# A decoder layer on one core: sums moved from GpSimd to VectorE, the norm's factor applied late, and two DeltaNet units beside the merge's loads

## The chip, the cores and the metric

One core of a Trainium2 chip runs the whole program. The time is that of one launch on the device, in microseconds (us). The engines are TensorE (PE, with PEld for its weight loads), VectorE (DVE), ScalarE (ACT), GpSimd (POOL) and SyncE (SP). In this kernel all transfers are issued by SP, in order.

## The reference

One layer of a decoder trunk with two mixers side by side, sequence 1024, width 1024, float32:

```
h   = RMSNorm(x);  p = h @ W_in
y_dn = GatedDeltaNet(p) @ W_dn      # 8 heads of 128, chunks of 64
y_ns = NSA(p) @ W_nsa               # 16 heads of 64; compressed, selected, window branches
x   = x + (sigmoid(g_dn) * y_dn + sigmoid(g_ns) * y_ns) @ W_out
x   = x + relu(RMSNorm(x) @ W_up)^2 @ W_down      # inner width 4096
```

RMSNorm(x) is x / sqrt(mean(x^2) + eps) * gain, over the width.

## The kernel before, in words

Activations lie transposed: the width on partitions, in 8 pieces c of 128, the sequence in two halves of 512. A matmul of two float32 operands is done as three: each operand is split into a high part (a copy by ScalarE, `wh`, `hh`, `ah`) and a low part (a subtraction on VectorE, `wl`, `hl`, `al`), and hi·hi, hi·lo and lo·hi go into the same PSUM bank. `split` (L184) and `parts` (L273) make the pair, `unit` (L280) loads two 128x512 tiles of weights and splits them. A scheduler puts the instructions of each engine in an order; priorities are the program's order and tables of steps (`at`, `at3`) where stages are mixed.

Start: x is loaded, made into hh and hl, and its squares are summed (`x_sums`, L334 and L335), partly on GpSimd. A root (`root_rows`, L244) takes eight one-column matmuls per row block, the mean on VectorE (L241), the power -1/2 on GpSimd (L242), a diagonal on VectorE (L252, `rd` or `tmp`) and a matmul that spreads it. Then come the DeltaNet heads, and the NSA attention with the DeltaNet output projection between its steps: `dn_part` multiplies, `dn_gate` (L1351 to L1353) loads a gate tile `th`, applies it and stores the result to `mxd`. The buffer `th` has one place, so the second gate is loaded after the first is stored.

Merge: `ns_rows` loads and splits the attention's rows `o`, `ns_merge` multiplies them with `w_pn`, gates the product and adds `mxd`'s tile (`md`). It can begin when the PSUM pools of the attention are shut and `pq` is opened. Output projection: `out_proj(half, c)`, 16 products, adds x, stores x1 (`x1d`), sums the squares. Norm: `norm_first` and `norm_second` multiply x1 by gain and root and form seven combinations of its four blocks, B11, B21, T2, T3, T4, T1, B22, each split in two.

MLP up and down use a Winograd scheme: a 2x2 block product in seven products p instead of eight. For the up product n = 0 to 15 and each product is 12 matmuls; `weights_of` makes the left side from the blocks a11, a12, a21, a22, two of its three sums on GpSimd (L1451 with no engine given, L1514); `up_out` applies relu and the square; `up_sums` forms the sums that the down product takes as its other side and stores them to `acd`. In the down product, 2 x 56 products are run in the order of `turns`, with sides prepared LEAD = 4 products ahead: w_d's blocks on the left, `acd`'s tiles (`bb`, split to `ah`, `al`) on the right, results added to x1 (L1664).

Of the kernel before, what the change touches and what calls it, by code (L numbers as in the profile page):

```python
# [146 lines left out]
def body(ctx: ExitStack, tc: tile.TileContext, A, out):  # L147
# [74 lines left out]
    for half in range(2):  # L222
        for k in range(8):
            xs.append(PL.pa.tile([128, 512], F32, name=f"x{half}{k}"))
            SY.dma_start(xs[-1], A["x"][k, :, half * 512:(half + 1) * 512])
        if half == 0:
            load_consts(cp, 0)
            cp_raw = [wp.tile([128, 4, 128], F32, name="wr", bufs=3) for _ in range(2)]
            for i in range(2):
                SY.dma_start(cp_raw[i], A["w_cp"][0][:, 4 * i:4 * i + 4])  # L230
# [49 lines left out]
    def unit(src):  # L280
        ks = []
        for i in range(2):
            wr = wp.tile([128, 4, 128], F32, name="wr", bufs=3)
# [42 lines left out]
    def x_sums(half):  # L326
        sa = [PL.pa.tile([128, 512], F32, name=f"sa{i}") for i in range(2)]
        for k in range(8):
# [5 lines left out]
            (GP if half or k >= 4 else V).tensor_tensor(sa[k // 4], sa[k // 4], sq, OP.add)  # L334
# [34 lines left out]
    for k in range(8):  # L369
        x_part(1, k)  # L370
    proj(p_cp, CX["w", 0], 0)
# [95 lines left out]
    def cmp_hidden(u, i):  # L467
# [3 lines left out]
        w1 = wp.tile([128, 4, 128], F32, name="wr", bufs=3)  # L471
# [72 lines left out]
    at(2, 2, cp_prep, 1)  # L544
# [371 lines left out]
    def fill_nb(u):  # L916
# [3 lines left out]
        def prep():  # L920
            for kp in range(4):
                wr = wp.tile([128, 2, 256], F32, name="wr", bufs=3)
# [415 lines left out]
    def dn_part(half, c, j):  # L1338
        oh, ol = D_["o", half]
        ks = D_["w", half, c]  # L1340
        if j == 0:
            D_["y"] = PL.ga.tile([128, 512], F32, name="g")
# [5 lines left out]
    def dn_gate(half, c):  # L1348
        sl = slice(half * 512, half * 512 + 512)
        th = PL.pr.tile([128, 512], F32, name="th", bufs=1)  # L1350
        SY.dma_start(th, gtd[c, :, sl])  # L1351
# [25 lines left out]
    shut("po", "pm", "pT", "pS", "ga", "pr")  # L1377
    pool("pf", 4, side="right")
    bank("pq", 4)
# [18 lines left out]
    def ns_merge(c, half):  # L1398
# [14 lines left out]
    ns_rows(0)  # L1413
    for c, half in [(0, 0), (1, 0), (0, 1), (1, 1)] + [(c, half) for c in range(2, 8) for half in range(2)]:
# [7 lines left out]
    x1, sums = [[], []], [None, None]  # L1422
# [3 lines left out]
    def out_proj(half, c):  # L1426
# [9 lines left out]
        SY.dma_start(x1d[c, :, HALF[half]], x)  # L1436
        if c == 0:
            sums[half] = t512(PL.p5, "u", 4)
            act(sums[half], x, AF.Square)
        else:  # L1440
            sq = t512(PL.pw, "tmp", 2)
            act(sq, x, AF.Square)
            (V if half else GP).tensor_tensor(sums[half], sums[half], sq, OP.add)
# [6 lines left out]
    def sub(o, a, b, eng=None):  # L1450
        (eng or GP).tensor_tensor(o, a, b, OP.subtract)  # L1451
# [3 lines left out]
    def parts_of(n, src, i, eng=V):  # L1455
        act(R[n][:, i], src)
        sub(R[n][:, 4 + i], src, f(R[n][:, i]), eng)

    def norm_first(r):
        R["raw"] = raw = f(big(False))  # L1460
        R["B11"], R["B21"] = big(True), big(True)
        for k in range(8):
            V.scalar_tensor_tensor(raw[:, k], x1[0][k], cols[:, 8 + k:9 + k], r, op0=OP.mult, op1=OP.mult)
            parts_of("B21" if k >= 4 else "B11", raw[:, k], k % 4)

    def norm_second(r):
        raw = R["raw"]
        R["T2"], R["T3"] = big(True), big(True)
        b12, b22, t = [], [], []

        def head(j):
            b12.append(t512(PL.p5, "b", 4))
            V.scalar_tensor_tensor(b12[j], x1[1][j], cols[:, 8 + j:9 + j], r, op0=OP.mult, op1=OP.mult)
            sub(raw[:, j], b12[j], raw[:, j], V)
            b22.append(t512(PL.p5, "c", 8))
            V.scalar_tensor_tensor(b22[j], x1[1][4 + j], cols[:, 12 + j:13 + j], r, op0=OP.mult, op1=OP.mult)

        def second(j):
            t.append(t512(PL.p5, "c", 8))
            sub(t[j], b22[j], raw[:, j], V)  # L1480
            parts_of("T2", t[j], j)

        head(0)
        for j in range(4):
            if j < 3:
                head(j + 1)
            second(j)
        yield
        for j in range(4):
            sub(b12[j], b22[j], b12[j])  # L1490
            parts_of("T3", b12[j], j)
        R["T4"], R["T1"] = big(False), big(False)
        for j in range(4):
            sub(raw[:, 4 + j], raw[:, 4 + j], t[j])
            parts_of("T4", raw[:, 4 + j], j)
        yield
        for j in range(4):
            parts_of("T1", raw[:, j], j)
        R["B22"] = big(False)
        for j in range(4):  # L1500
            parts_of("B22", b22[j], j, GP)
        yield

    def weights_of(blocks, p, home):

        a11, a12, a21, a22 = [blocks.get(b) for b in ("a11", "a12", "a21", "a22")]
        if p == 6:
            t = t512(home, "tmp", 2)
            sub(t, a22, a11, V)
# [3 lines left out]
        if p == 5:  # L1513
            GP.tensor_tensor(a21, a21, a22, OP.add)  # L1514
# [34 lines left out]
    def up_out(n, p, x):  # L1549
        act(x, x, AF.Relu)  # L1550
        act(x, x, AF.Square)
        H[n, p] = x
# [5 lines left out]
    def up_sums(n):  # L1558

        b11, b21, b22, b12 = [H.pop((n, p)) for p in (1, 2, 3, 0)]  # L1560
        sub(b11, b12, b11, V)
        t = t512(PL.p5, "c", 8)
        sub(t, b22, b11, V)
# [47 lines left out]
    LAST = {7: "a11", 3: "a12", 5: "a21", 4: "a22"}  # L1611
# [3 lines left out]
    def down_load(n, i, b):  # L1615
        if n < NC:
            k = 2 * (J * n + i)
            m, d = int(b[1]) - 1, int(b[2]) - 1
            DW[n, i, b] = t = t512(PL.pg if d == 0 else PL.ph, b, J)
# [8 lines left out]
    def down_prep(q):  # L1628
# [6 lines left out]
        if n and p == 1:  # L1635
            sub(w["a11"], w["a11"], w["a21"])
        e = q - J - 5
        if 0 <= e < J:
            sub(DW[0, e, "a11"], DW[0, e, "a11"], DW[0, e, "a21"])
# [28 lines left out]
    for half, c in [(half, c) for c in range(CB) for half in range(2)] + [(half, c) for half in range(2) for c in range(CB, 8)]:  # L1668
        out_proj(half, c)
        if (half, c) == (1, CB):  # L1670
            norm_first(root(0))
# [79 lines left out]
```

## Time and profile before

| | us |
|---|---|
| runs of before | 2408.16, 2409.52, 2412.6 (median 2409.52) |
| profiled execution, its own time | 2409.07 |
| its span | 2407.3 |
| TensorE busy | 2339.8 (97%) |
| VectorE busy | 1563.8 (65%) |
| ScalarE busy | 1093.4 (45%) |
| GpSimd busy | 569.0 (24%) |

The stages by the span's clock: start to about 45 us, DeltaNet to 1080, attention to 1590, merge to 1650, output projection and norm to 1800, MLP up to 2115, MLP down to the end. In a row of the timeline stand start, duration, engine, line, operation, output and inputs with their shape, and in brackets the idle time of the engine before it with what ended it. "x3" joins three like instructions. A row of waits reads: who waited, for which line of which engine; total us, times, longest. Line numbers are those of the kernel before.

### The profile page before, as it was taken

The numbers are of one execution on the slowest core, as the hardware profiler recorded it, in microseconds if no ns is written. First come the engines' busy times: TensorE is split into PE (matmuls) and PEld (weight loads), VectorE is DVE, ScalarE is ACT, GpSimd is POOL, SyncE is SP. The second block draws the span as 40 slices with busy tenths as digits, with TensorE's granted clock in tenths as the row PEclk, the third lists the DMA queues.
The fourth block names the chain that finished last, engine by engine and source line by source line (L and its number), as shares of the span: only waits on it lengthen the run. The fifth ranks groups of instructions, "written<-read, shape, count | busy, mean of one in ns | idle before, by whom it ended". The sixth has DMA issues, their size and how long they took to land. (4 is left out here: it accounts for less than half of the span.)

```text
span 2407.3 us, 44378 instructions
## 1 busy us (share of the span) xinstructions
PE 2339.8 (97%) x16673; PEld 1916.8 (80%) x16673; DVE 1563.8 (65%) x3626; ACT 1093.4 (45%) x2258; POOL 569.0 (24%) x473
## 2 busy tenths in 40 slices
PE   7999999999999999999999999999999999989999
PEld 5887878787878887877777777778878888878887
DVE  6766664747484838348877777643397666596785
ACT  4233343434344444227666766532355555534443
POOL 3132321203231423000010111012145444260320
PEclk9999999999999999999999999999999999999999
DMA  5421313131212221237432422164425443566333
GB/s 176 135 65 56 85 43 94 42 91 44 80 50 82 51 77 50 87 116 179 131 115 72 115 89 73 32 225 161 148 83 172 144 149 136 204 232 225 109 126 102
DMA packets 237510, 267.37 MB, mean 111 GB/s; under 512 B 76976, under 2 KB 128496, under 8 KB 237168
## 3 DMA queue, kind: packets, MB, share of 16 engines
q1 hardware_dynamic: 237296, 264.55, 35.2%
q8 instruction: 131, 2.15, 0.4%
q14 instruction: 83, 0.68, 0.1%
HBM read 190.05 MB, written 72.38 MB: 109 GB/s over the span
## 5 line engine op out<-in xcount | busy, mean ns | idle before, releaser
L177 PE MATMUL g<-hh,wh 128*128 128x512 f32 (+1 forms) x816 | 335.4, 411 | 8.2 <-ACT hh L174 7.3
L177 PE MATMUL g<-hl,wh 128*128 128x512 f32 (+1 forms) x816 | 327.4, 401 | 0.1
L177 PE MATMUL g<-hh,wl 128*128 128x512 f32 (+1 forms) x816 | 323.5, 396 | 0.0
L177 PE MATMUL V<-big,wh 128*128 128x512 f32 x768 | 239.4, 392 | 1.6 <-DVE c L1594 1.6
L186 DVE TENSOR_TENSOR wl<-a,wh 128x512 fp32r<-128x512 f32 x192 | 160.6, 838 | 111.0 <-ACT wh L174 110.9
L174 ACT ACTIVATE wh<-wr 128x512 fp32r<-128x512 f32 x210 | 132.1, 630 | 207.1 <-PE g L177 131.4
L174 ACT ACTIVATE wh<-a 128x512 fp32r<-128x512 f32 x192 | 121.1, 631 | 219.6 <-PE V L177 109.5
L1223 DVE CUSTOM_DVE_ANT_0 junk<-S,cst 128x384 f32<-128x384 f32 (+3 forms) x320 | 168.4, 533 | 56.8 <-PE S L177 52.7
L277 DVE TENSOR_TENSOR wl<-wr,wh 128x512 fp32r<-128x512 f32 x178 | 123.6, 698 | 111.9 <-ACT wh L174 108.4
L177 PEld LDWEIGHTS g<-hh,wh 128*128 128x128 f32 (+1 forms) x816 | 153.6, 188 | 36.2 <-ACT hh L174 7.5
L174 ACT ACTIVATE P<-T 128x512 f32<-128x512 f32 x228 | 134.0, 597 | 100.9 <-PE T L177 88.9
L177 PEld LDWEIGHTS g<-hh,wl 128*128 128x128 f32 (+1 forms) x816 | 153.4, 188 | 29.5 <-issue 0.6
L177 PEld LDWEIGHTS g<-hl,wh 128*128 128x128 f32 (+1 forms) x816 | 153.8, 188 | 26.4 <-DVE hl L324 0.8
L177 PEld LDWEIGHTS V<-big,wh 128*128 128x128 f32 x768 | 144.7, 189 | 32.7 <-ACT c L174 1.2
L177 PE MATMUL V<-big,wl 128*128 128x512 f32 x384 | 150.5, 392 | 3.2 <-DVE wl L186 3.2
L177 PE MATMUL g<-wh,hh 128*128 128x256 f32 x512 | 147.4, 288 | 0.0
L177 PE MATMUL g<-wl,hh 128*128 128x256 f32 x512 | 144.8, 283 | 0.0
L177 PE MATMUL g<-wh,hl 128*128 128x256 f32 x512 | 144.8, 283 | 0.0
L1272 POOL TENSOR_TENSOR acc<-acc,bs 128x256 f32<-128x256 f32 x62 | 48.9, 789 | 401.3 <-DVE bs L1270 286.9
L177 PEld LDWEIGHTS o<-vv,P 128*64 128x64 f32 x3648 | 116.0, 138 | 27.1 <-issue 20.4
L177 PE MATMUL o<-vv,P 128*64 128x65 f32 x3648 | 130.1, 225 | 0.0
L177 PE MATMUL S<-ks,qc 96*128 96x384 f32 (+3 forms) x320 | 127.1, 409 | 1.6 <-DVE mx L1223 1.4
(371 smaller groups left out, 5709.1 us busy)
## 6 DMA issues: line engine op xcount, KB each, us to landing
bb<-acd SPq DMA_DIRECT2D x112, 256.0 KB, 2.8
wr<-in_w_dn_dram SPq DMA_DIRECT2D x64, 256.0 KB, 2.9
a<-in_w_u_dram SPq DMA_DIRECT2D x64, 256.0 KB, 3.4
acd<-c SPq DMA_DIRECT2D x64, 256.0 KB, 3.0
a<-in_w_d_dram SPq DMA_DIRECT2D x64, 256.0 KB, 4.9
wr<-in_w_nb_dram SPq DMA_DIRECT2D x32, 256.0 KB, 2.7
wr<-in_w_gt_dram SPq DMA_DIRECT2D x32, 256.0 KB, 2.7
gtd<-fx SPq DMA_DIRECT2D x32, 256.0 KB, 2.2
```

Of the source, the lines that this page charges most:

```text
L174: return SC.activation(o, i, fn, **kw)
L177: return PE.matmul(o, l, r, start=start, stop=stop, skip_group_check=True)
L186: V.tensor_tensor(lo, src, f(hi), OP.subtract)
L277: V.tensor_tensor(wl, wr, f(wh), OP.subtract)
L1223: V.tensor_tensor_reduce(junk[:, :w], ps[:, :w], mask[:, a:b], 1.0, 3e38, OP.add, OP.min, o)
L1272: adds.tensor_tensor(acc, acc, b, OP.add)
```

## The change

- Start: all sums of squares are on VectorE. The second compressed unit is loaded and split after the second half of hh and hl, ahead of the first root, instead of at a step of the DeltaNet stage. Its raw tiles lie in another pool; after that pool is shut, `unit` uses two places of the MLP's "a22" tiles instead of three of "wr".
- Merge: the DeltaNet output units c = 6 and 7 of the second half come out of the attention's table and after `ns_rows(0)`, each with its own gate tile, loaded ahead; the attention's pools are shut after them. md + th is on VectorE.
- Norm: `out_proj` makes x1 times gain on ScalarE. The root is one matmul with a matrix of ones, a mean and a RECIPROCAL of 128x512 on VectorE; relu(r·y)^2 is r^2·relu(y)^2, so the factor 1/mean is multiplied in `up_out` after the square. The differences of the blocks need no root and are made inside the output projection's second half.
- MLP: all sums are on VectorE.
- Down: the first block runs the products in the order 4, 2, 1, 5, 6, 3, 7, a22 is loaded first, and loads follow that order.

```diff
-            (GP if half or k >= 4 else V).tensor_tensor(sa[k // 4], sa[k // 4], sq, OP.add)
+            V.tensor_tensor(sa[k // 4], sa[k // 4], sq, OP.add)
...
+    CX["w", 1] = unit(A["w_cp"][1])
     proj(p_cp, CX["w", 0], 0)
     x_root(0, sa)
...
+            if hasattr(PL, "pw"):
+                wr = PL.pw.tile([128, 512], F32, name="a22", bufs=2).rearrange("p (a b) -> p a b", a=4)
+            else:
+                wr = PL.cq.tile([128, 4, 128], F32, name="wr", bufs=3)
...
-                e = 22 + 2 * c
+                at3(e - 0.5, dn_weights, half, c)
+                continue
...
-        GP.tensor_tensor(md, md, th, OP.add)
+        V.tensor_tensor(md, md, th, OP.add)
...
+    ths = []
+    for c in (6, 7):
+        ths.append(t512(PL.pw, "a12"))
+        SY.dma_start(ths[-1], gtd[c, :, HALF[1]])
     ns_rows(0)
+    for c in (6, 7):
+        for j in range(4):
+            dn_part(1, c, j)
+        dn_gate(1, c, ths[c - 6])
+    shut("po", "pm", "pT", "pS", "ga", "pr")
...
+        act(y, x, AF.Copy, scale=cols[:, 8 + c:9 + c])
...
     def root(half):
-        return root_rows(sums[half], PL.pq, "Q", PL.pw, PL.p5.tile([128, 4], F32, name="r4", bufs=1), 2)
+        p = t512(PL.pq, "Q")
+        mm(p, K("ones"), sums[half], True, True)
+        rr[half] = r = sums[half]
+        V.tensor_scalar(r, p, 1.0 / D, EPS, op0=OP.mult, op1=OP.add)
+        V.reciprocal(r, r)
...
-        (eng or GP).tensor_tensor(o, a, b, OP.subtract)
+        V.tensor_tensor(o, a, b, OP.subtract)
...
+    def norm_second(j):
+        sub(raw[:, j], b12[j], raw[:, j])
+        t2s.append(t512(PL.p5, "u", 4))
+        sub(t2s[j], b22[j], raw[:, j])
+        sub(b12[j], b22[j], b12[j])
+        sub(raw[:, 4 + j], raw[:, 4 + j], t2s[j])
...
-            GP.tensor_tensor(a21, a21, a22, OP.add)
+            V.tensor_tensor(a21, a21, a22, OP.add)
...
         act(x, x, AF.Square)
+        r = rr[p in (0, 3)]
+        V.tensor_tensor(x, x, r, OP.mult)
...
-    turns = [(1, 2, 6, 5, 7, 3, 4), (2, 1, 5, 6, 3, 7, 4)]
+    turns = [(4, 2, 1, 5, 6, 3, 7), (2, 1, 5, 6, 3, 7, 4)]
...
+            down_load(0, q - 8, "a11")
             down_load(0, q - 8, "a21")
...
-                down_load(0, i, "a11")
+                down_load(0, i, "a22")
```

Three places in the order of the engines. The first is SP's queue at the entry of the merge (gtd holds the gates, ond the attention's rows, mxd the gated DeltaNet output). Before, the weights w_pn came early and each gate after the store of the one ahead:

```order
L284 DMA wr<-in_w_pn_dram 128x512
L1353 DMA mxd<-th 128x512
L284 DMA wr<-in_w_pn_dram 128x512
L1351 DMA th<-gtd 128x512
L1282 DMA ond<-ot 128x2x128 x3
L1395 DMA a_18952<-ond 128x512
```

And with the change:

```order
L1418 DMA a_18880<-gtd 128x512
L1396 DMA a_18882<-ond 128x512
L1396 DMA a_18886<-ond 128x512
L1396 DMA a_18890<-ond 128x512
L1396 DMA a_18894<-ond 128x512
L1357 DMA mxd<-a_18878 128x512
L1396 DMA a_18898<-ond 128x512
L1396 DMA a_18902<-ond 128x512
L1396 DMA a_18906<-ond 128x512
L1396 DMA a_18910<-ond 128x512
L1357 DMA mxd<-a_18880 128x512
L287 DMA a_18984<-in_w_pn_dram 128x512
```

Both gates now come ahead of the rows, and the first tile of w_pn stands behind the store of the second gated tile.

The second is VectorE at the end of the output projection, in the change alone (L1478 are the differences, L1465 sums of squares, L1451 x plus the product, L277 the splits of w_o's last unit):

```order
L1478 TENSOR_TENSOR big<-big 128x512 x4
L1451 TENSOR_TENSOR c<-c,V 128x512
L1478 TENSOR_TENSOR big<-big 128x512
L1472 TENSOR_SCALAR s_19690<-Q 128x512
L1478 TENSOR_TENSOR big<-big 128x512
L1465 TENSOR_TENSOR s_19723<-s_19723,tmp 128x512
L1473 RECIPROCAL s_19690<-s_19690 128x512
L1451 TENSOR_TENSOR c<-c,V 128x512
L277 TENSOR_TENSOR wl<-a_20227,wh 128x512
L277 TENSOR_TENSOR wl<-a_20233,wh 128x512
```

The RECIPROCAL, which was not there, stands with ten other operations ahead of two splits.

The third is the left side of the down product. Before, GpSimd made three sums per index at p = 6:

```order
L1451 TENSOR_TENSOR a_22950<-a_22950,a_23199 128x512
L1514 TENSOR_TENSOR a_23199<-a_23199,a_23201 128x512
L1451 TENSOR_TENSOR a_23073<-a_23073,tmp 128x512
L1451 TENSOR_TENSOR a_22954<-a_22954,a_23225 128x512
L1514 TENSOR_TENSOR a_23225<-a_23225,a_23227 128x512
```

With the change they stand on VectorE, between its splits, from p = 1 on:

```order
L186 TENSOR_TENSOR wl<-a_23247,wh 128x512
L1478 TENSOR_TENSOR a_23247<-a_23247,a_23249 128x512
L186 TENSOR_TENSOR al<-bb,ah 128x512
L1515 TENSOR_TENSOR a_23249<-a_23249,a_22995 128x512
L1478 TENSOR_TENSOR tmp<-a_22995,a_23247 128x512
L186 TENSOR_TENSOR wl<-a_23273,wh 128x512
L186 TENSOR_TENSOR al<-bb,ah 128x512
L1478 TENSOR_TENSOR a_23273<-a_23273,a_23275 128x512
L1478 TENSOR_TENSOR a_23121<-a_23121,tmp 128x512
```

The three sums of one index are now spread over two products' splits.

More of the change, by code (lines that the diff above doesn't have):

```diff
@@ L227, in body @@
             load_consts(cp, 0)
-            cp_raw = [wp.tile([128, 4, 128], F32, name="wr", bufs=3) for _ in range(2)]
+            cp_raw = [PL.cq.tile([128, 4, 128], F32, name="wr", bufs=3) for _ in range(2)]
             for i in range(2):
@@ L1341, in dn_part @@
         if j == 0:
-            D_["y"] = PL.ga.tile([128, 512], F32, name="g")
+            D_["y"] = PL.pT.tile([128, 512], F32, name="T") if half and c == 7 else PL.ga.tile([128, 512], F32, name="g")
         for k in (2 * j, 2 * j + 1):
@@ L1346, in dn_part, with dn_gate @@
             mm(D_["y"], ks[k][1], oh[:, k], False, k == 7)
-    def dn_gate(half, c):
+    def dn_gate(half, c, th=None):
         sl = slice(half * 512, half * 512 + 512)
-        th = PL.pr.tile([128, 512], F32, name="th", bufs=1)
-        SY.dma_start(th, gtd[c, :, sl])
+        if th is None:
+            th = PL.pr.tile([128, 512], F32, name="th", bufs=1)
+            SY.dma_start(th, gtd[c, :, sl])
         V.scalar_tensor_tensor(th, th, 1.0, D_["y"], op0=OP.add, op1=OP.mult)
@@ L1420, in body @@
     pool("p5")
-    x1, sums = [[], []], [None, None]
+    x1, sums, rr = [[], []], [None, None], [None, None]
+    raw, b12, b22, t2s = f(big(False)), [], [], []
     CB = 3
@@ L1436, in out_proj @@
         SY.dma_start(x1d[c, :, HALF[half]], x)
+        if half == 0:
+            y = raw[:, c]
+        else:
+            y = t512(PL.p5, *(("b", 4) if c < 4 else ("c", 8)))
+            (b12 if c < 4 else b22).append(y)
+        act(y, x, AF.Copy, scale=cols[:, 8 + c:9 + c])
         if c == 0:
-            sums[half] = t512(PL.p5, "u", 4)
+            sums[half] = t512(PL.p5, f"s{half}", 1)
             act(sums[half], x, AF.Square)
@@ L1504, in weights_of, with norm_parts @@
+    def norm_second(j):
[4 more added lines that the diff above has]
+        sub(raw[:, 4 + j], raw[:, 4 + j], t2s[j])
+    def norm_parts(n):
+        R[n] = big(n in ("T2", "T3"))
+        parts_of(n, {"T2": t2s, "T3": b12, "T4": [raw[:, 4 + j] for j in range(4)],
+                     "T1": [raw[:, j] for j in range(4)], "B22": b22}[n])
     def weights_of(blocks, p, home):
@@ L1508, in weights_of @@
             t = t512(home, "tmp", 2)
-            sub(t, a22, a11, V)
+            sub(t, a22, a11)
             src = t
@@ L1607, in body @@
     J, NC = 8, 2
[L1608 removed]
+    turns = [(4, 2, 1, 5, 6, 3, 7), (2, 1, 5, 6, 3, 7, 4)]
     dorder = [(n, i, p) for n in range(NC) for p in turns[n] for i in range(J)]
     ADDS = {1: [(0, 0)], 2: [(0, 0)], 6: [(0, 1)], 4: [(1, 0)], 7: [(1, 0), (1, 1)], 5: [(1, 1)], 3: [(0, 1)]}
[L1611 removed]
+    LAST = {7: "a11", 3: "a12", 5: "a21", 6: "a22"}
     RING = 6
@@ L1634, in down_prep @@
         split(DB.pop(q), ah, al)
-        if n and p == 1:
+        if p == 1:
             sub(w["a11"], w["a11"], w["a21"])
-        e = q - J - 5
-        if 0 <= e < J:
-            sub(DW[0, e, "a11"], DW[0, e, "a11"], DW[0, e, "a21"])
         G_[n, i, p] = wgt, (ah, al)
@@ L1670, in body @@
         if (half, c) == (1, CB):
-            norm_first(root(0))
+            root(0)
+            norm_first()
+        if half and c >= 4:
+            norm_second(c - 4)
+    norm_parts("T2")
     todo = list(order)
@@ L1706, in body @@
     for q in range(len(order)):
-        if q == 2:
-            second = norm_second(root(1))
-        if q in (2, 7, 8):
-            next(second)
+        if q in (2, 4, 6, 8):
+            norm_parts(("T3", "T4", "T1", "B22")[q // 2 - 1])
+        if q == 3:
+            root(1)
         prepare(q + 1 + LEAD if q < END_U else max(len(order), q + LEAD), ahead)
```

82 lines of the change are left out of this document (22 added, 60 removed).

## The prediction

> **What bounds the kernel now.** I read first the busy shares on the page, then what TensorE waited for, then the stretches around each wait, and last single rows of the timeline.
>
> ```profile
> PE 2339.8 (97%) x16673; PEld 1916.8 (80%) x16673; DVE 1563.8 (65%) x3626; ACT 1093.4 (45%) x2258; POOL 569.0 (24%) x473
> ```
>
> TensorE (PE) is busy for 2339.8 of 2407.3 us. The change leaves its matmuls alone but for a few, so what can be won is the other 67.5 us, and what the clock costs after a stall. The view of TensorE's waits names the late engines (total us, times, longest):
>
> ```profile
> PE g L177 <- ACT hh L174: 7.3, 1, 7.3
> PE Q L177 <- DVE al L186: 6.0, 3, 2.2
> PE V L177 <- issue: 4.9, 1, 4.9
> PE s L177 <- DVE rd L252: 3.7, 2, 3.1
> PE V L177 <- DVE wl L186: 3.2, 1, 3.2
> PE V L177 <- DVE c L1594: 1.6, 2, 0.8
> PE Q L177 <- DVE tmp L252: 1.6, 1, 1.6
> PE Q L177 <- DVE c L1476: 1.2, 1, 1.2
> ```
>
> The first is the load of x, which nothing here touches. The others lie in four places that the diff touches: start, merge, norm, and the passage from MLP up to MLP down. The stretches around them, and the steady part of the up product (us; busy us of PE, PEld, DVE, ACT, POOL; granted clock; DMA share; GB/s):
>
> ```profile
> 0.00:45.00 45.00, 32.33 (x129) 20.83 (x130) 28.23 (x43) 25.20 (x44) 16.84 (x19) 0.96 0.45 153
> 1570.00:1600.00 30.00, 24.35 (x156) 19.30 (x152) 16.07 (x28) 11.39 (x19) 1.31 (x1) 0.89 0.63 203
> 1768.00:1820.00 52.00, 45.17 (x184) 35.24 (x184) 50.05 (x60) 30.90 (x55) 34.98 (x23) 0.93 0.19 65
> 1850.00:2080.00 230.00, 230.00 (x1016) 190.47 (x1015) 144.06 (x168) 127.65 (x214) 92.81 (x59) 1.00 0.40 138
> 2114.00:2160.00 46.00, 38.83 (x154) 30.57 (x153) 40.76 (x35) 14.95 (x27) 40.78 (x24) 0.93 0.56 197
> ```
>
> Each troubled stretch has a second cost beside its idle time: the granted clock falls. Length x (1 - clock) is 1.8 us at the start, 3.3 at the merge, 3.6 at the norm and 3.2 at the passage. In the steady stretch TensorE never stops: a 512-wide matmul takes 230/1016 = 0.226 us, a product of 12 takes 2.72, the seven products of one n take 19.07.
>
> **Passage to the down product.** In p = 6 each product has three sums on GpSimd, and VectorE's next difference waits for the last of them:
>
> ```profile
> 2122.05 1.80 POOL L1514 TENSOR_TENSOR a<-a,a 128x512 f32<-128x512 f32 x1
> 2127.28 0.69 DVE L1451 TENSOR_TENSOR tmp<-a,a 128x512 f32<-128x512 f32 x1 [1.18 <-POOL a L1451]
> 2127.32 1.80 POOL L1514 TENSOR_TENSOR a<-a,a 128x512 f32<-128x512 f32 x1
> 2140.22 0.59 PE L177 MATMUL Q<-al,wh 128*128 128x512 f32 x1 [2.23 <-DVE al L186]
> 2152.27 0.49 PE L177 MATMUL Q<-al,wh 128*128 128x512 f32 x1 [2.00 <-DVE al L186]
> ```
>
> From 2122.05 to 2127.32 this chain gives one product per 5.27 us, while TensorE needs one per 2.72. Once the products prepared ahead are spent TensorE stops: 46.00 - 38.83 = 7.2 us idle and 3.2 by the clock, 10.4 in all. The change puts the sums on VectorE and runs the products as 4, 2, 1, 5, 6, 3, 7. What VectorE takes for a sum beside a silent GpSimd is seen where the norm ends: 1764.99 - 1764.39 = 0.60 us from start to start.
>
> ```profile
> 1764.39 0.69 DVE L186 TENSOR_TENSOR wl<-a,wh 128x512 fp32r<-128x512 f32 x1
> 1764.99 0.69 DVE L1443 TENSOR_TENSOR u<-u,tmp 128x512 f32<-128x512 f32 x1
> ```
>
> In p = 6 VectorE then has at most 36 operations (split of both sides, tmp, the sums, x sums) x 0.605 = 21.8 us for eight products of 2.72 = 21.8 us. That is no margin, but four products are prepared ahead and p = 4, 2, 1 before it need only two to five per product. I take a gain of 9.5; the ends are 5 (VectorE runs out in p = 6 or p = 1, and half the stall stays) and 10.4.
>
> DMA could be the next thing late there, since a11 and a21 now come one product apart while p = 2 runs: three pieces of 256 KB per product and half an x1 tile, 0.92 MB in 2.72 us = 337 GB/s. Before, the stretch ahead of this one moved
>
> ```profile
> 2080.00:2114.00 34.00, 33.22 (x147) 27.18 (x146) 25.22 (x36) 19.77 (x34) 3.75 (x3) 1.00 1.01 361
> ```
>
> 361 GB/s at full queues with 0.8 us of idle TensorE. So 337 fits, barely, and each piece has eight products to land; I put nothing for it.
>
> **Start.** All sums of squares go to VectorE, and the second compressed unit's split comes before the first root.
>
> ```profile
> 15.85 4.11 POOL L334 TENSOR_TENSOR sa<-sa,sq 128x512 f32<-128x512 f32 x3 [14.05 <-ACT sq L174]
> 19.99 0.69 DVE L335 TENSOR_TENSOR sa<-sa,sa 128x512 f32<-128x512 f32 x1 [3.93 <-POOL sa L334]
> 15.16 1.66 ACT L174 ACTIVATE sq<-x 128x512 f32<-128x512 f32 x3
> 20.60 7.47 DVE L324 SCALAR_TENSOR_TENSOR hl<-x,cols,hh 128x512 fp32r<-128x512 f32 x8
> 26.79 0.45 PE L177 MATMUL c<-hl,wh 128*64 128x512 f32 x1 [0.77 <-DVE hl L324]
> 31.08 2.07 PE L177 MATMUL s<-rd,cst 128*128 128x512 f32 x2 [3.13 <-DVE rd L252]
> ```
>
> VectorE idled 3.93 us for three GpSimd sums of 1.37. ScalarE has the last square at 15.16 + 1.66 = 16.82, and the sums follow the squares as they come, so the last ends near 17.5, and hl starts 2.5 us earlier or more. Its eight rows, 7.47/8 = 0.93 each beside GpSimd, take about 0.67 each without it (the 0.60 above and a little for the third operand). Two splits, the mean, GpSimd's power (now at once) and rd follow: rd is ready near 26. The matmul that waits for it is moved eight matmuls later, to 27.8. So the waits for rd (3.13), for hl (0.77, and 0.26 of a like one) and for sa (0.56), and 1.7 of slow clock go: -6.4. Ends: -4, if the next squares queue ahead of rd, and -8, if the second root's wait shrinks too. The weights that are split early are no new wait: they were asked for at the same place before, and lay in SBUF when they were split.
>
> **Merge.** Before, GpSimd is no part of it. The second gate tile was asked for only when the first one's store let its buffer go:
>
> ```profile
> 1584.47 0.32 SPq L1351 DMA_DIRECT2D th<-gtd  x1
> 1589.17 0.69 DVE L1352 SCALAR_TENSOR_TENSOR th<-th,g 128x512 f32<-128x512 f32 x1 [1.11 <-DMA th<-gtd]
> 1589.96 1.19 PE L177 MATMUL V<-o,wh 128*128 128x512 f32 x2 [4.86 <-issue]
> ```
>
> Now both gates are loaded early, so their multiplications wait only for TensorE, done near 1584.1. But the merge's weights, which lay in SBUF before, now stand in SP's queue behind the store of that last gate, and in a two-deep ring. The gate itself stands behind some of the row splits on VectorE, so the store is issued at 1585 to 1586.5, the weights 0.4 to 0.8 us later; they take 2.5 us (usual for this size in the page's DMA issues) to 4.5 (the tile above, 1584.47 to 1589) to land, and 1.3 to be split. TensorE starts at 1589.5 to 1592.5 instead of 1589.96: one wait replaced by another of the same length. I take +1.5. Ends: -3 (loads land in 2.5 us and the earlier 0.78 us wait for the first gate goes) and +5 (the second half-unit and the clock add to it). The sum md + th on VectorE costs nothing: 0.60 us under each product of 24 matmuls, 5.4 us.
>
> **Norm.** The reciprocal root as it was (eight matmuls of one column, GpSimd's power, a diagonal, a matmul) becomes one matmul and a mean and a RECIPROCAL of the whole 128x512 on VectorE; the factor is applied after the squares of the up product.
>
> ```profile
> 1744.46 0.95 PE L177 MATMUL Q<-cst,u 128*128 128x1 f32 x8
> 1745.27 0.72 PE L177 MATMUL V<-big,wh 128*128 128x512 f32 x2
> 1795.03 1.75 DVE L186 TENSOR_TENSOR wl<-a,wh 128x512 fp32r<-128x512 f32 x1
> 1796.84 0.79 PE L177 MATMUL V<-big,wl 128*128 128x512 f32 x1 [3.16 <-DVE wl L186]
> 50.74 0.55 DVE L419 RECIPROCAL s<-s 128x64 f32<-128x64 f32 x1
> 1570.70 0.18 DVE L1266 RECIPROCAL coef<-o 128x4 f32<-128x4 f32 x1 [9.05 <-PE o L177]
> ```
>
> Less on TensorE: two times 1745.27 - 1744.46 = 0.81, so -1.6. The stalls of this stretch were 52.00 - 45.17 = 6.8 us and 3.6 by the clock; the second counts some idle time again, so I take 9.7. VectorE was busy 50.05 of 52 us there, with rows of 1.75 beside GpSimd; now most differences run inside the output projection, at 0.60. What is new is the RECIPROCAL on an in-order engine. By the two rows it grows by (0.55 - 0.18)/60 = 6.1 ns an element: 3.3 us for 512; in proportion to the larger row it is 4.4. I take 3.3, as the slope leaves the fixed part out. Around the first one ten other operations (6.0 us) and it stand ahead of the split that TensorE needs: 9.3 to 10.4 us, against a lead of four half-units of 2.72 = 10.9 less 1.3 for landing in two engines. So 0 to 1.6 us stay there, and 0.5 at the product after the output projection's last. From the second RECIPROCAL to the split for the first p = 6 product stand nine more rows (5.4 us), 8.7 together, against a lead of two to three products, 5.4 to 8.2: about 2 us. With 4.5 left of 9.7, the gain is 5.2; ends 0 and 9.4.
>
> The Trainium skill's VectorE: DVE Perf Modes, "First, the fixed hardware budget", says that a reciprocal is an iterative divide with a repeat count of 8. An estimate from that page (512 x 8 cycles at 0.96 GHz) is 4.27 us for each, which speaks against this edit: two of them would add 1.9 us to VectorE and take the sum from -21.7 to some -20. The small rows here (0.55 for 64) agree with 8 cycles an element (0.53); no run so far shows 512 of them.
>
> **Up product.** VectorE gets all four sums of a weight unit, four multiplications by the root's factor and four sums of results: 23 operations per n, 23 x 0.605 = 13.9 us under TensorE's 19.07. Before it had 14 and GpSimd five, at these prices:
>
> ```profile
> L186 DVE TENSOR_TENSOR wl<-tmp,wh 128x512 fp32r<-128x512 f32 x12 | 21.4, 1785 | 0.0
> L1594 DVE TENSOR_TENSOR u<-u,V 128x512 f32<-128x512 f32 x12 | 8.3, 688 | 19.9 <-PE V L177 19.9
> ```
>
> TensorE had no idle time to give back, so the edit is worth nothing, or 0.5 at n = 14 (the waits for c). I take -0.5.
>
> **Sum**, against the profiled execution's own 2409.07 (2407.3 of span and 1.8 around it; 0.5 under the median of the runs): -6.4 + 1.5 - 5.2 - 1.6 - 0.5 - 9.5 = -21.7, and 2387.4.
>
> **Rivals.**
> Only the passage is won: the RECIPROCALs and the merge's weights cost what start and norm bring. For it: VectorE's order has no margin at either. Against it: the start's gain depends on neither. Start -4, merge +5, norm -1.6 alone, passage -7: 2401.
> VectorE becomes the bound of the up product. It has an in-order queue in which each multiplication now waits for ScalarE's square, which waits for TensorE, and splits for later products stand behind. Its point is 19.07/23 = 0.83 us an operation, waits included. The merge shows such a wait for ScalarE:
>
> ```profile
> 1583.16 1.32 DVE L186 TENSOR_TENSOR o<-a,o 128x512 fp32r<-128x512 f32 x2 [0.31 <-ACT o L174]
> ```
>
> With 0.31 us of it on each operation, 0.605 + 0.31 = 0.915, one n takes 21.04 instead of 19.07, and 16 of them 31 us more, which ends slower than before: 2418. Against it: four products of lead, and PSUM inputs do not slow VectorE (688 ns above).
> Nothing visible: weights in the merge come 8 us late, since the ring is shared and two deep, and the passage only loses a third. -4 + 8 - 1.6 - 3 = 2408.
>
> **How the numbers follow.** Forecast 0.70, only the passage 0.16, nothing 0.07, VectorE as the bound 0.07. A change under 0.2%, 4.8 us, can't be told from none. Faster is the forecast and the first rival, 0.86, written 0.85, since that rival could be larger; the same is the third with this hundredth, 0.08; slower 0.07. Range: the four sizable terms' ends, if they fall independently, give 8 us about the forecast, 2379 to 2396; the first rival takes it to 2401. I write 2377 to 2401.
>
> **What would show it.** Right: in the passage TensorE's stops for al and wl are gone, and GpSimd has no sum left in the MLP. At the start rd's wait is under 0.5 us. At the merge TensorE waits for the weights (wh or wl from the a22 tiles) instead of the gate, 4 to 7 us. In the norm the RECIPROCAL takes 3.3 or 4.3 us, with one wait of 1 to 3 us behind each. Wrong: VectorE over 90% busy between 1850 and 2080, TensorE waiting there for wl, or a wait of over 3 us in p = 1 of the down product.

## The result and the profile after

The changed kernel takes 2389.39 us (median of four runs, 2388.47 to 2393.95) against 2409.17 for the kernel before: ratio 0.9919, 95% interval 0.9902 to 0.9936. The forecast was 2387.4 in 2377 to 2401. The profiled execution took 2389.25 us, its span is 2387.5, so that stages can be compared span to span (-19.8 us). Medians and ranges below leave out the one execution, of the last kernel of the merge's experiments, that took 9.4 ms.

The page of the changed kernel, its first line on engines:

```profile
PE 2331.2 (98%) x16657; PEld 1913.1 (80%) x16657; DVE 1602.5 (67%) x3846; ACT 1102.2 (46%) x2274; POOL 292.6 (12%) x299
```

GpSimd lost half of its busy time, yet VectorE, with 220 operations more, gained only 39 us: its operations became shorter (a split beside a GpSimd sum took up to 1.79 us before, now 0.69). The view of TensorE's waits, cut to the places that the change touches:

```profile
PE V L177 <- ACT wh L174: 9.7, 2, 8.7
...
PE s L177 <- DMA wr<-in_cw_dram: 2.2, 1, 2.2
...
PE Q L177 <- DVE wl L186: 1.6, 2, 1.2
...
PE V L177 <- DVE wl L277: 0.9, 1, 0.9
PE c L177 <- DVE gb L510: 0.8, 1, 0.8
PE V L177 <- DVE c L1597: 0.8, 1, 0.8
...
PE s L177 <- DVE rd L252: 0.6, 1, 0.6
```

The waits for al (6.0 us), for tmp and for the norm's c are gone, that for rd fell from 3.7 to 0.6. One is new: 8.7 us for the split of the merge's first weights, where the kernel before waited 4.9. One grew: the wait for a load of cw1, from 0.7 to 2.2 us. The stretches (us; busy us of PE, PEld, DVE, ACT, POOL; granted clock; DMA share; GB/s):

```profile
0.00:45.00 45.00, 36.98 (x156) 25.34 (x157) 34.15 (x61) 25.88 (x46) 6.97 (x15) 1.00 0.57 185
45.00:100.00 55.00, 50.79 (x273) 42.63 (x272) 36.03 (x72) 10.58 (x24) 2.74 (x4) 0.94 0.54 156
1570.00:1600.00 30.00, 21.34 (x102) 17.11 (x98) 15.53 (x26) 12.20 (x21) 0.00 (x0) 0.89 0.73 240
1745.00:1820.00 75.00, 71.76 (x308) 57.04 (x308) 73.35 (x114) 44.12 (x80) 0.00 (x0) 1.00 0.31 108
1850.00:2070.00 220.00, 220.00 (x973) 182.15 (x972) 167.03 (x262) 122.93 (x207) 0.00 (x0) 1.00 0.37 135
2106.00:2152.00 46.00, 46.00 (x204) 38.10 (x203) 39.99 (x65) 20.68 (x36) 0.00 (x0) 1.00 0.92 323
```

The passage to the down product (last row) has no idle time and the full clock. The norm has 3.2 us idle at full clock. The start's first 45 us are better by 4.7 us of busy TensorE, but the slow clock has moved into the next stretch. The merge is worse.

The same matmuls, found in both traces by their place in TensorE's order, give each stage's share. The numbers are their starts in the span:

| matmul | before | after | lead | gained in the stage |
|---|---|---|---|---|
| first of the attention (S from ks, qc) | 1092.33 | 1090.11 | 2.22 | start and DeltaNet: 2.2 |
| first of the DeltaNet output projection | 1120.86 | 1118.81 | 2.05 | -0.2 |
| last of the merge | 1678.95 | 1679.30 | -0.35 | attention and merge: -2.4 |
| last of the up product | 2086.36 | 2078.59 | 7.77 | output projection, norm, up: 8.1 |
| 17th product of down (first matmul of ah and wl) | 2130.56 | 2122.79 | 7.77 | 0 |
| 25th product of down, the same | 2163.83 | 2144.55 | 19.28 | the third eight products: 11.5 |
| end | 2407.30 | 2387.47 | 19.83 | 0.55 |

### The profile page after: what moved, and what is told of

It reads as the page before. It is cut to its first block, busy times and chain, and to the rows that moved or that the text cites. A ratio compares the mean times of both kernels' runs of the same rounds, so it can differ in the third digit from the quotient of the medians.

```text
span 2387.5 us, 44217 instructions
## 1 busy us (share of the span) xinstructions
PE 2331.2 (98%) x16657; PEld 1913.1 (80%) x16657; DVE 1602.5 (67%) x3846; ACT 1102.2 (46%) x2274; POOL 292.6 (12%) x299
## 4 chain that ended last, share of the span: by engine, by line
PE 84%; DVE 8%; DMA 3%; POOL 2%; issue 2%; ACT 1%; SPq 0%; DVEq 0%; POOLq 0%; ACTq 0%
PE g L177 30%; PE V L177 19%; PE Q L177 12%; PE T L177 5%; PE o L177 5%; PE s L177 4%; PE c L177 3%; PE S L177 3%; PE m L177 1%; DVE acc L676 1%; DMA ab<-asc 1%; DMA a<-ond 1%; DVE St L849 1%; PE tp L609 1%; PE m L1280 0%
## 5 line engine op out<-in xcount | busy, mean ns | idle before, releaser
L174 ACT ACTIVATE wh<-a 128x512 fp32r<-128x512 f32 x234 | 146.8, 629 | 248.6 <-PE V L177 150.0
L186 DVE TENSOR_TENSOR wl<-a,wh 128x512 fp32r<-128x512 f32 x192 | 131.9, 689 | 72.4 <-ACT wh L174 72.3
L174 ACT ACTIVATE wh<-wr 128x512 fp32r<-128x512 f32 x168 | 105.7, 629 | 155.2 <-PE g L177 127.5
L277 DVE TENSOR_TENSOR wl<-wr,wh 128x512 fp32r<-128x512 f32 x136 | 94.9, 702 | 90.7 <-ACT wh L174 89.6
L676 DVE SCALAR_TENSOR_TENSOR acc<-xp,cols,acc 128x512 f32<-128x512 f32 x144 | 117.0, 813 | 6.3 <-ACT acc L174 4.8
```

The lines of the kernel that those rows point to most:

```text
L174: return SC.activation(o, i, fn, **kw)
L186: V.tensor_tensor(lo, src, f(hi), OP.subtract)
L277: V.tensor_tensor(wl, wr, f(wh), OP.subtract)
L676: V.scalar_tensor_tensor(a2, xp[:, i:i + 512], cols[:, c0 + i:c0 + i + 1], a2, op0=OP.mult, op1=OP.add)
```

## The experiments

Medians below come from several sets of runs, each with the kernel before beside it (2410 to 2412 us), so that ratios are to be compared and, for parts of a us, the stage clocks of the profiled executions. One thing varies between executions of any kernel here: TensorE's first matmul, which waits for x, came between 6.2 and 8.2 us.

### The start: a cw1 buffer of its own

First the rows of the changed kernel, on TensorE and on SP, that made this experiment:

```profile
27.97 1.12 PE L177 MATMUL s<-rd,cst 128*128 128x512 f32 x2
55.23 1.16 PE L177 MATMUL s<-cx,wr 128*128 128x126 f32 x8 [2.21 <-DMA wr<-in_cw_dram]
51.74 0.48 SPq L448 DMA_DIRECT2D gcd<-gct  x1
52.31 1.01 SPq L476 DMA_DIRECT2D wr<-in_cw_dram  x2
```

The last matmul ahead of that wait in the changed kernel, then the same matmul and the store of gct in the kernel before:

```profile
52.62 0.40 PE L177 MATMUL g<-hh,wl 128*128 128x512 f32 x1
58.69 0.39 PE L177 MATMUL g<-hh,wl 128*128 128x512 f32 x1
56.45 0.48 SPq L444 DMA_DIRECT2D gcd<-gct  x1
```

The first root's matmul does come at 27.97 us without a wait, 3.1 us earlier, and at 52.62 us TensorE is 6.1 us ahead of the kernel before. Then it needs cw1's tiles, which SP issues at 52.31, behind the store of gct at 51.74, and gct hangs on a chain of the gates on VectorE and ScalarE that came only 4.7 us earlier (56.45 before). Behind the wait the lead is 4.6 us. Then the granted clock is 0.50 for 6.8 us, and at 64 us the lead is 2.3:

```profile
56.66:63.49 6.83, 6.66 (x19) 5.58 (x20) 6.63 (x10) 1.85 (x4) 0.52 (x1) 0.50 0.67 196
```

```diff
-        w1 = PL.cq.tile([128, 4, 128], F32, name="wr", bufs=3)
+        w1 = PL.pb.tile([128, 4, 128], F32, name="w1", bufs=1) if i == 3 else PL.cq.tile([128, 4, 128], F32, name="wr", bufs=3)
```

> The changed kernel, but the last of each group of four cw1 tiles has a buffer of its own, so that its load need not wait for one of the three shared ones and can be issued ahead of the store of gct. Theory A (the start gave back what the sums on VectorE had won because TensorE, 6 us ahead, ran into the load of cw1, 2.2 us, and the halved clock that followed, 2 us): the wait before the matmuls on cx and wr shrinks from 2.21 us to under 0.5, no slow clock near 60 us, the attention begins 3 to 4 us earlier than in the changed kernel (1090.1), total 2385 to 2387. Theory B (the DeltaNet stage is bound by VectorE's chain, and a lead at its entry is lost anyway): the wait goes but the attention begins within 1 us of 1090.1, total as before it, 2389.

Measured: 2382.00 us (2380.51 to 2384.45), ratio 0.9878, interval 0.9863 to 0.9893; span 2382.7. The attention begins at 1084.12, 6.0 us earlier than in the changed kernel, of which 0.95 is the first matmul's. SP now issues the tile ahead of the store, the wait is gone and so is the slow clock of the stretch after it (1.00 for 0.94):

```profile
48.20 0.35 SPq L476 DMA_DIRECT2D wr<-in_cw_dram  x1
45.00:100.00 55.00, 52.89 (x314) 45.95 (x313) 40.36 (x80) 13.35 (x30) 2.98 (x4) 1.00 0.58 170
```

So theory A holds, and is exceeded: it put the attention 3 to 4 us earlier and the total at 2385 to 2387. The start's gain had been won and was given back at the load. The lead is kept through DeltaNet and attention.

### The start: the sums and the early split, one at a time

Both on top of the kernel above, so that the load does not hide what they are worth.

```diff
-            V.tensor_tensor(sa[k // 4], sa[k // 4], sq, OP.add)
+            (GP if half or k >= 4 else V).tensor_tensor(sa[k // 4], sa[k // 4], sq, OP.add)
```

> The changed kernel with the cw1 buffer of its own (2382 us), and the sums of squares at the start back on GpSimd as they were. If the sums were worth what the prediction put for the start, the first root's matmul comes back from 27.5 to 31 us with its wait and slow clock, and the total is 4 to 6.5 us longer: 2386 to 2389. If the early split of the second unit brought most of it, only 0 to 2 us longer.

Measured: 2389.16, ratio 0.9916 (0.9900 to 0.9933), span 2387.0 against 2382.7. The wait is back at the first root:

```profile
32.84 2.08 PE L177 MATMUL s<-rd,cst 128*128 128x512 f32 x2 [4.76 <-DVE rd L252]
```

The attention begins 5.4 us later and the span is 4.3 longer; 1.1 of either is that TensorE's first matmul came later here. So in the profiled executions the sums on VectorE are worth 3.2 to 4.3 us. The medians differ by more, 7.2 us, and the execution of the kernel above that was profiled is the slowest of its four. That the sums account for a large part of the start's gain is shown; whether they are worth less or more than the 6.4 us of the prediction is not.

```diff
-    CX["w", 1] = unit(A["w_cp"][1])
...
+    at(2, 2, cp_prep, 1)
```

> The changed kernel with the cw1 buffer of its own (2382 us), and the second compressed unit loaded and split at its old place. If the early split only moves work, 0 to 1 us. If, as the order of SP's queue says, its raw tiles then hold two of three buffers for longer, the cw1 loads come behind the store of gct again, the wait before the matmuls on cx and wr is back (2 us, and a slow clock after it), and the total is 3 to 5 us longer: 2385 to 2387.

Measured: 2388.59, ratio 0.9912 (0.9898 to 0.9927), span 2385.5, 2.9 us more than with the early split, 1.5 of it the later first matmul. The two waits that the early split spares:

```profile
53.43 1.16 PE L177 MATMUL s<-cx,wr 128*128 128x126 f32 x8 [1.73 <-DMA wr<-in_cw_dram]
57.62 0.50 PE L177 MATMUL g<-hh,wh 128*128 128x512 f32 x1 [2.14 <-DVE cx L358]
```

No slow clock followed these, and the attention began only 0.8 us later beyond the first matmul's 1.5. The wait for the load of cw1 is back, as expected of raw tiles that hold the shared buffers longer; the wait for cx was not. The total lies above the 2385 to 2387 that were expected, and the medians differ by more (6.6 us) than the spans do; how much the early split is worth, 1.4 us or more, is not settled by this.

### The merge: what TensorE waits for

The rows of the changed kernel, on SP, ScalarE and TensorE:

```profile
1581.14 2.19 SPq L1396 DMA_DIRECT2D a<-ond  x4
1583.60 0.32 SPq L1357 DMA_DIRECT2D mxd<-a  x1
1583.97 0.90 SPq L287 DMA_DIRECT2D a<-in_w_pn_dram  x2
1588.92 1.27 ACT L174 ACTIVATE wh<-a 128x512 fp32r<-128x512 f32 x2 [1.36 <-DMA a<-in_w_pn_dram]
1589.60 1.22 PE L177 MATMUL V<-o,wh 128*128 128x512 f32 x2 [8.66 <-ACT wh L174]
```

The weights are issued right behind the gate's store, as predicted, and land near 1588.9. TensorE's last DeltaNet matmul ended at 1580.9. The first experiment moves those two loads to the front of the queue; the split comes after unit 6's gate.

```diff
+    for i in range(2):
+        pn0.append(t512(PL.pw, "a22", 2).rearrange("p (a b) -> p a b", a=4))
+        SY.dma_start(pn0[i], A["w_pn"][0][:, 4 * i:4 * i + 4])
     for c in (6, 7):
         ths.append(t512(PL.pw, "a12"))
...
         dn_gate(1, c, ths[c - 6])
+        if c == 6:
+            ks[0] = parts(pn0[0]) + parts(pn0[1])
```

> The changed kernel with one edit: the two tiles of the first w_pn unit are loaded ahead of the two gates and of the attention's rows, and split after the gate of unit 6, so that they no longer stand in SP's queue behind the store of the last gate. Theory A (that queue place is what keeps TensorE idle for 8.66 us at the merge): TensorE resumes near 1583 to 1585 instead of 1589.6, the idle time falls to 2 to 4 us, total 2383 to 2385, 5 to 6 us less than the changed kernel. Theory B (the rows of the attention, of which the last four are split only near 1588, would stop it anyway): it resumes early but stops again for the rows, and 1 to 3 us are won, total 2387.

Measured: 2389.81 (2387.33 to 2391.00), ratio 0.9906 (0.9890 to 0.9923), span 2389.2: nothing won, a miss for the totals of both theories. TensorE resumes at 1585.06, 4.5 us earlier, for now the rows are the last to come; and it stops again:

```profile
1582.33 2.60 ACT L174 ACTIVATE o<-a 128x512 fp32r<-128x512 f32 x4 [4.59 <-DMA a<-ond]
1587.94 5.69 SPq L1396 DMA_DIRECT2D a<-ond  x4
1593.68 0.90 SPq L287 DMA_DIRECT2D a<-in_w_pn_dram  x2
1598.24 1.22 PE L177 MATMUL V<-o,wh 128*128 128x512 f32 x2 [4.17 <-ACT wh L174]
```

SP needs 5.69 us for four loads of the second half's rows, because their ring of four frees one place per split; the weights of the next unit stand behind them. The wait had moved down the queue by one unit: theory B was right that TensorE would stop again, but it stopped for weights.

The second experiment undoes the merge part.

```diff
             if half and c >= 6:
-                at3(e - 0.5, dn_weights, half, c)
-                continue
+                e = 22 + 2 * c
...
-    for c in (6, 7):
-        for j in range(4):
-            dn_part(1, c, j)
-        dn_gate(1, c, ths[c - 6])
```

> The changed kernel with the merge part undone: DeltaNet units 6 and 7 of the second half are back in the attention's table, with the one shared gate buffer; the first w_pn unit still uses the two-deep ring, opened after the attention. If the new place of the two units cost 3.5 us, as the two traces' clocks at the merge suggest (the lead of 3.1 us before it was a lag of 0.35 us after it), this kernel is 2 to 4 us faster than the changed one, near 2386. Rival: the weights, which come late in both, are the cost, and the units' place none or a gain: same or slower, 2389 to 2393.

Measured: 2384.68 (2382.64 to 2388.91), ratio 0.9891 (0.9876 to 0.9905), span 2383.8, 3.7 us less than the changed kernel, as the first of the two theories had it. TensorE waits less, although for the same one-buffer gate as before the change:

```profile
1576.10 0.50 PE L177 MATMUL g<-oh,wh 128*128 128x512 f32 x1 [0.78 <-DVE th L1356]
1585.44 1.19 PE L177 MATMUL V<-o,wh 128*128 128x512 f32 x2 [3.59 <-issue]
```

Over all profiled executions, the time from the first matmul of the DeltaNet output projection to the last of the merge tells the two forms apart: 556.6 to 558.1 us in the four with the old form (the kernel before, this one, and two below), 560.2 to 562.6 in the six with the new one unaltered. The means, 557.5 and 561.3, put the cost of the merge part at 3.9 us.

Both first edits together:

> Both edits together: the cw1 buffer of its own and the early first w_pn unit. If the two are independent, their gains add: 8 to 10 us under the changed kernel, 2379 to 2382. If the lead won at the start is lost in the DeltaNet stage, only that of the merge remains: 2383 to 2385.

Measured: 2384.47, ratio 0.9886 (0.9872 to 0.9901), span 2382.2. The attention begins at 1084.05 as with the buffer alone, and the early weights again bring nothing (4.1 us of waiting at the second unit). The gain is that of the start. The total falls into the range of the second theory by chance, for that theory had the gain of the merge remain.

Next the second unit's weights are moved ahead of the rows too, with the cw1 buffer kept:

```diff
         if (c, half) == (1, 0):
+            ks[1] = unit(A["w_pn"][1])
             ns_rows(1)
```

> The changed kernel with the cw1 buffer, the first w_pn unit loaded ahead of gates and rows, and the second w_pn unit loaded ahead of the second half's rows (its tiles, behind those rows, cost 4.1 us of waiting when only the first was moved). If SP's queue is all that keeps the new merge slow, that second wait goes too: 2377 to 2379, as good as undoing the merge part or better. If the rows themselves, through their ring of four, are late, under 2 us against 2382.

Measured: 2379.56 (2375.16 to 2386.08), ratio 0.9870 (0.9851 to 0.9889), span 2377.8. The second wait shrinks to less than 1 us at a time:

```profile
1577.24 1.14 PE L177 MATMUL V<-o,wh 128*128 128x512 f32 x2 [2.98 <-ACT o L174]
1583.67 0.50 PE L177 MATMUL V<-o,wh 128*128 128x512 f32 x1 [0.23 <-DVE o L186]
1586.15 0.73 PE L177 MATMUL V<-o,wh 128*128 128x512 f32 x2 [0.71 <-ACT wh L174]
1587.56 0.80 PE L177 MATMUL V<-o,wl 128*128 128x512 f32 x1 [0.67 <-DVE wl L277]
```

The stretch to the merge's last matmul takes 558.1 us by the measure above, as in the old form. With the cw1 buffer and the first unit alone moved it was 561.8. So the order of SP's queue was the cost: with both weight units ahead of the rows the new form is as good as the old one, and no better: TensorE then waits 2.98 us for the rows.

The cw1 buffer with the merge part undone, for comparison:

> The changed kernel with the cw1 buffer of its own and the merge part undone, the two edits that each took 4 to 5 us off. If they are independent: 2378 to 2380. If the merge, reached earlier, waits longer for its loads, 2381 to 2382, no better than with the buffer alone.

Measured: 2380.50 (2379.61 to 2382.45, three executions), ratio 0.9875 (0.9859 to 0.9890), span 2377.8. The two edits add in the span (4.8 and 3.7 off 2387.5 would be 2379.0). The median lies between the ranges of the two theories and does not part them.

### The passage: the engine or the order

The change did two things there. Each alone:

```diff
-            V.tensor_tensor(a21, a21, a22, OP.add)
+            (V if home is PL.pw else GP).tensor_tensor(a21, a21, a22, OP.add)
...
-            sub(a12, a12, t)
+            (V if home is PL.pw else GP).tensor_tensor(a12, a12, t, OP.subtract)
...
-            sub(w["a11"], w["a11"], w["a21"])
+            GP.tensor_tensor(w["a11"], w["a11"], w["a21"], OP.subtract)
```

> The changed kernel with the three sums of the down product's left side back on GpSimd (a11 - a21 at p = 1, a21 + a22 at p = 5, a12 - tmp at p = 6); the new order of the products stays. Theory 'engine' (three GpSimd sums per product, 1.7 to 1.8 us each, are what was too slow): in the new order each phase has only one of them, 1.8 us for 2.72, but VectorE's operations beside them take up to 1.75 us again, so that some stalls of 1 to 5 us return, total 2390 to 2394. Theory 'order' (what helped is that the three sums no longer fall into one phase): within 2 us of the changed kernel's 2389. If more than 8 us return, a GpSimd sum is bad in any order.

Measured: 2393.13 (2391.08 to 2396.47), ratio 0.9932 (0.9916 to 0.9947), span 2389.6. The third eight products of down take 24.11 us, against 21.76 in the changed kernel and 33.27 before. VectorE is slowed again, to 1.77 us for a split that takes 0.69 in the changed kernel, but what is left of the stalls is small and the clock stays full:

```profile
2106.00:2152.00 46.00, 44.84 (x194) 35.86 (x193) 40.78 (x42) 19.07 (x34) 30.39 (x18) 1.00 0.79 278
2130.03 1.77 DVE L186 TENSOR_TENSOR wl<-a,wh 128x512 fp32r<-128x512 f32 x1
2133.55 0.50 PE L177 MATMUL Q<-al,wh 128*128 128x512 f32 x1 [0.38 <-DVE al L186]
2129.52 1.74 POOL L1639 TENSOR_TENSOR a<-a,a 128x512 f32<-128x512 f32 x1
2132.91 1.74 POOL L1639 TENSOR_TENSOR a<-a,a 128x512 f32<-128x512 f32 x1
```

The total is the one that theory 'engine' gave. Its picture of one GpSimd sum per phase is not what the trace shows: for several products GpSimd makes two (L1515 and L1639 in turn), one product in 3.4 us, where it made three in 5.27 before and TensorE needs 2.72.

And the kernel before, its left sides' sums on VectorE, in the old order:

```diff
-            GP.tensor_tensor(a21, a21, a22, OP.add)
+            V.tensor_tensor(a21, a21, a22, OP.add)
...
-            sub(a12, a12, t)
+            sub(a12, a12, t, V)
...
-            sub(w["a11"], w["a11"], w["a21"])
+            sub(w["a11"], w["a11"], w["a21"], V)
...
-            sub(DW[0, e, "a11"], DW[0, e, "a11"], DW[0, e, "a21"])
+            sub(DW[0, e, "a11"], DW[0, e, "a11"], DW[0, e, "a21"], V)
```

> The kernel before, with one thing of the change: the three sums of the left side in MLP up and down are on VectorE (those of the norm and of the results stay on GpSimd), in the old order of the products. In p = 6 VectorE then has six operations of 0.605 us for 2.72 us of TensorE, 3.63; over eight products it falls 7.3 us behind, and four products of lead are 10.9. Theory 'engine': the passage's stalls go nearly all, 8 to 11 us, total 2398 to 2401. Theory 'order': the lead is used up before, half of the stalls stay, total 2403 to 2406.

Measured: 2401.59 (2398.55 to 2404.10), ratio 0.9965 (0.9952 to 0.9978), span 2400.4. The third eight products take 21.77 us. No idle time is left in the passage, though VectorE makes six operations per product in p = 6:

```profile
2114.00:2160.00 46.00, 46.00 (x205) 38.09 (x204) 44.70 (x74) 20.30 (x35) 0.00 (x0) 1.00 0.90 309
```

So theory 'engine' holds for the passage with 11.5 us, the lead of four products covering VectorE, which is busy for 97% of these 46 us. But 'order' without 'engine', in the experiment ahead of this one, gives 9.2 of them. Either cures the stall, wholly or nearly; they do not add. The total is just above the 2398 to 2401 of theory 'engine'. In this kernel the norm and up product, whose other sums stay on GpSimd, take 321.3 us from the first up matmul to the last, 3.0 more than before, with a wait of 1.99 us for VectorE's wl near 1816.9 that the kernel before has not. That more operations on VectorE beside a GpSimd that still works are the cost there is likely, but no run shows it apart.

### The norm: the price of RECIPROCAL

The rows of the changed kernel on VectorE and TensorE:

```profile
1748.03 3.35 DVE L1473 RECIPROCAL s<-s 128x512 f32<-128x512 f32 x1
1752.67 0.50 PE L177 MATMUL V<-big,wl 128*128 128x512 f32 x1 [0.93 <-DVE wl L277]
1785.09 3.35 DVE L1473 RECIPROCAL s<-s 128x512 f32<-128x512 f32 x1
1793.46 0.73 PE L177 MATMUL Q<-big,wh 128*128 128x512 f32 x2 [0.48 <-ACT wh L174]
```

```diff
         V.tensor_scalar(r, p, 1.0 / D, EPS, op0=OP.mult, op1=OP.add)
-        V.reciprocal(r, r)
```

> The changed kernel without the two RECIPROCALs of the norm: the factor applied after the squares is then the mean square itself, not one over it; all else is as it was. It measures the price of two 3.35 us instructions on VectorE's queue. Theory A (the waits left in the norm, 0.93 us at the last w_o unit, 1.19, 0.48, 0.41 and 0.24 in the first products, stand behind them): 2 to 3 us less than the changed kernel's 2389, and those waits gone. Theory B (the waits come from the many sums around them): under 0.5 us less.

Measured: 2385.42 (2383.34 to 2386.82), ratio 0.9893 (0.9879 to 0.9907), span 2384.1. From the last matmul of the merge to the last of the up product it is 394.65 us for 399.29 (398.7 to 399.4 in all ten kernels here that have the RECIPROCALs whole), so the two are worth 4.6 us, more than the 3.2 us of waits in which they showed. Of the stretch nothing is idle any more:

```profile
1745.00:1820.00 75.00, 75.00 (x328) 61.27 (x327) 72.04 (x119) 49.56 (x89) 0.00 (x0) 1.00 0.38 128
```

Theory A holds, and is exceeded. Is it the length of one instruction, or the load on VectorE? On top of the kernel with both weight units moved:

```diff
-        V.reciprocal(r, r)
...
+    def inverse(half, i):
+        r = rr[half][:, i * 128:(i + 1) * 128]
+        V.reciprocal(r, r)
...
+        if half and c >= 4:
+            inverse(0, c - 4)
...
+        if 4 <= q < 8:
+            inverse(1, q - 4)
```

> The kernel of the last three edits (own cw1 buffer, both first w_pn units ahead of the rows; 2377.8 us of span) with each RECIPROCAL of 128x512 cut into four of 128x128, spread over the following steps of the output projection and of the up product, so that splits can stand between them. By the slope of 6.1 ns an element one takes about 0.93 us, four 3.7 in all, more than the one of 3.35. Theory 'latency' (what TensorE waits for in the norm is the 3.35 us for which nothing else passes on VectorE): the waits of this stretch, 3.2 us before, fall under 1, and 2 to 4.6 us are won (4.6 is what leaving the two out won): 2373 to 2376. Theory 'load' (VectorE is 98% busy there, and any 6.7 us more stop TensorE): within 1 us of 2378.

Measured: 2377.43 (2375.38 to 2379.51), ratio 0.9864 (0.9847 to 0.9880), span 2376.9, 0.9 us less; from the merge's last matmul to the up product's last 397.05 for 398.73, 1.7 us less. The eight pieces, and the stretch around them:

```profile
L1487 DVE RECIPROCAL s<-s 128x128 f32<-128x128 f32 x8 | 7.6, 953 | 0.0
1735.00:1810.00 75.00, 73.40 (x318) 59.05 (x317) 74.83 (x122) 46.30 (x83) 0.00 (x0) 1.00 0.33 112
```

The first wait, at w_o's last unit, is gone: that one was length. From the merge's last matmul to the up product's first it is 87.92 us, the same as without the RECIPROCALs, and 89.16 to 89.24 in the ten kernels that have them whole. The later waits stayed (0.95 and 0.41 us), with VectorE busy for 74.83 of 75 us: those look like load. The up product takes 308.9 us, 306.5 without the RECIPROCALs and 309.3 to 310.0 with them whole. By the total, theory 'load' is the nearer one: 2377.43 lies within 1 us of 2378 and outside 2373 to 2376. This is the fastest kernel measured, by 0.55% of the kernel before under the changed one; it and the one it is built on can't be told apart by their intervals.

## Why the prediction was right, point by point

The total was 2 us off, but single terms were off by up to 4, in opposite senses. That they offset each other so well is luck.

- **Passage, -9.5 put, -11.5 measured** (and 0.55 at the later wait near 2294). The mechanism was right: GpSimd's three sums per product were the chain, VectorE does them in 0.69 us, and the lead covers what it falls behind. The term was undersized twice: the stall itself was 11.5 us (33.27 for 21.76), beyond the 10.4 read from idle time and clock, and 0.9 was kept back for stalls of VectorE, which was busy for 87% of the stretch and caused none. The prediction did not see that the order of the products would nearly do alone. DMA, held possible at 337 GB/s, moved 323 without a wait.
- **Start, -6.4 put, -2.2 measured.** The step that failed is "So the waits ... and 1.7 of slow clock go: -6.4". They went (rd's matmul at 27.97, put at 27.8; 6.1 us of lead at 52.62 us). What was missing is what comes next: the load of cw1 behind the store of gct on SP, a wait that grew from 0.71 to 2.21 us (the lead fell to 4.6), and a slow clock that came back 1.4 us behind it (the lead fell to 2.3). The prediction asked what would be late next on VectorE's queue, not on SP's. With that load given a buffer the attention begins 8.2 us earlier than in the kernel before, 1.1 of it the first matmul's.
- **Merge, +1.5 put, +2.4 measured between the two profiled executions**, 3.9 over all with each form. The step was right: the weights behind the last gate's store took the place of the gate's own load. TensorE's start was put at 1589.5 to 1592.5 and was 1589.6, which is partly luck: the last gate's store came at 1583.60, earlier than the 1585 to 1586.5 that were put, and the first weights took longer to land, 4.9 us from 1583.97 to the split at 1588.92, put at 2.5 to 4.5. But TensorE had been through with DeltaNet at 1580.9, not 1584.1, being ahead, so its wait was 8.7 us, beyond the 4 to 7 that were named; and a second wait of 1.05 us, at the next unit, was in the bounds only.
- **Norm, -5.2 and -1.6, and up, -0.5: -7.3 put, -8.1 measured.** The RECIPROCAL takes 3.35 us, put at 3.3 by the slope of two rows. What is left of the stalls was put at 4.5 us, though the three waits that were named add up to 2.5 to 4.1; taking the RECIPROCALs out won 4.6, in idle time and in what does not show as idle. The saving of 1.6 on the roots' matmuls was not measured apart. The three waits had been named at their places with 0 to 1.6, 0.5 and 2 us; those seen were 0.93, 1.19 and 1.13 (0.48, 0.41, 0.24 together). By the Trainium skill's VectorE: DVE Perf Modes, "First, the fixed hardware budget", the estimate had been 4.27 us each. The trace does not agree with that estimate: 3.35.
- **The rivals.** VectorE did not become the bound of the up product: 167.0 of 220 us busy (76%), TensorE never idle, the predicted 13.9 us under 19.07 being 73%. "Only the passage is won" has its part of the truth at start and merge, but the norm paid.

So the forecast was right by its largest term and by the norm. Without the passage's surplus of 2.5 us, which offset part of the start's shortfall, it would have been some 4 us too low.

## What to carry to other kernels

When a stall goes away early in a program, look on every queue, the DMA queue first, for the next thing that hangs on an older chain: here a lead of 6 us met a load that stood behind a store. When work is moved so that a wait disappears, list the transfers that are now issued behind it: the merge's weights behind stores and rows in an in-order queue cost 4 us, and moving the first unit of them ahead brought nothing until the second was moved too. And when two edits cure one stall, try each alone: the second may be free to be dropped, or may have a price elsewhere.

## What the runs showed of the hardware

- RECIPROCAL on VectorE: 3.35 us for 128x512, 0.95 for 128x128, 0.18 for 128x4, so 6.2 ns an element between the first two, while a sum of 128x512 takes 0.69.
- A granted clock of 0.50 followed a wait of 2.21 us on TensorE (55.23; from 56.7 to 63.5), and likewise waits of 2.18 to 2.35 at that place in the four other kernels that have it. None followed waits of 1.73 and 2.14 at nearly the same place in another kernel. But the length of a wait is not all: from 1105 to 1112 us the clock was 0.54 in the changed kernel, where no wait in the 20 us ahead was over 0.7 us. What decides stays open.
- With GpSimd silent, no VectorE sum of 128x512 in the up product and the passage took more than 0.69 us in the mean (before: up to 1.79), at a DMA share of 0.37 and at 0.92 alike. With GpSimd's sums back, splits took 1.77 again.
